# A hybrid four-layer model on one core: the order of every engine from one plan over the whole program

## The chip, the cores and the metric

The kernel runs on one core of a Trainium2 chip. The metric is the device time of one execution in microseconds; the time before is the median of three runs, and one further execution was profiled. The core's engines are TensorE (matrix products), VectorE, ScalarE, GpSimd and SyncE, which here issues DMAs. Each works through its own queue in order; semaphores tie them together.

## The reference

A sequence of 256 tokens, 1024 wide, in float32, goes through two blocks of two layers each. Both layers of the first block project the normalised x to the inputs of three mixers (a recurrence, an attention over 64 selected keys, dilated attention), multiply their joined output by `w_out`, and then add a gated projection of a second input `p`:

```
for i in range(2):                                   # first block
    z = rms_norm(x, norm_g[i]) @ w_in[i]
    y = concat(rwkv7(z_a), sparse_attention(z_b), dilated(z_c))
    x = x + y @ w_out[i]
    x = x + sigmoid(rms_norm(x, ple_norm_g[i]) @ ple_w_gate[i]) * (p[i] @ ple_w_proj[i])
x = rms_norm(x, final_norm_g)
for l in range(2):                                   # second block
    h = rms_norm(x, attn_norm[l])
    o = compressed/selected/window attention (l = 0) or attention with decay (l = 1), and attention to mem
    x = x + o @ w_o[l]
    u = conv3(rms_norm(x, ffn_norm[l]) @ w_up[l]) + conv_b[l]      # 2 x 2816 columns
    x = x + (silu(u[:, :2816]) * u[:, 2816:]) @ w_down[l]
return rms_norm(x, final_norm)
```

The recurrence of `rwkv7` (six heads, a 64 x 64 state each) is computed in four chunks of 64 tokens.

## The kernel before

**Products.** A float32 product is made of three products in a faster type: each operand x is split into a high half (a rounded copy) and a low half (x minus the copy), and hi·hi, hi·lo and lo·hi are added in PSUM (`mm3`, `PASSES`). TensorE therefore gets three matmuls of 128 x 128 weights by 256 or 512 columns for each tile of a projection. Small products (attention, the recurrence, transposes) run as plain float32.

**Weights.** A `Load` brings weights from DRAM through a ring of three raw tiles of 512 KB (`wraw`, `RBUFS`). ScalarE writes the high half of each block (`whi`), VectorE or, for every n-th block, GpSimd the low half (`wlo`); each has a ring of six (`WBUFS`). `Chain`s link the loads, so that the next projection's weights are fetched and split while the current one runs. Activations are split in the same way (`put_pair`, `stack_row`); in the feed-forward stage GpSimd makes the low half of the gated product (`k<-yv,k`).

**Stages.** `flow.run(...)` is called nine times: mixers and gated projection for each layer of the first block, mixers and feed-forward for each layer of the second, and the last norm. A call takes several Python generators (streams): the dense projections, the norms' statistics, the recurrence, the attentions. The feed-forward stage has 11 passes a layer, each with two up-projections of 256 columns and the down-projection of the pass before.

**Order of TensorE.** Streams are interleaved by `Flow`, which keeps a clock of its own: `Clock` estimates when VectorE, ScalarE, GpSimd and DMA finish each operation (`RATE`), and `Flow.run` resumes the first stream in its list whose operands it thinks are ready. A stream that has handed work over waits for it with a margin: `PACE` holds, for each of the nine calls, a margin of 0.15 to 0.6 us and a lag between TensorE and the others of 0.2 to 0.28, and three places add 2.0 to 3.5 us (`GN_LAG`, `GRAM_LAG`, `SPREAD_LAG`). The order in which this program emits matmuls is kept as it is by `tc.manual_schedule(engines={PE})` (line 494).

**Order of the other engines.** VectorE, ScalarE, GpSimd and SyncE are ordered by the framework's scheduler, which has estimates of its own (`schedule_with_timeline_sim=True`). It also gives each tile a slot of its pool and places the semaphores.

**The norms.** Row sums of squares give 1/rms by three Newton steps on [128, 1] tiles, mostly on GpSimd (`newton`: `rs_t`, `rs_y`). `spread_rs` spreads the two columns of scales over the partitions: VectorE writes a diagonal tile (`diag`), and TensorE multiplies it by ones.

Nearly every instruction has the line of a helper: 458 for all engines but TensorE, 616 for matmuls, 621 for transposes.

## Time and profile before

| what | us |
|---|---|
| median of three runs (1206.95 to 1211.45) | 1207.41 |
| the profiled execution | 1210.38 |
| its span, first to last instruction | 1208.6 |
| TensorE, matmuls busy | 1111.5 |
| TensorE, weight loads busy (beside the matmuls) | 988.7 |
| VectorE busy | 913.0 |
| ScalarE busy | 716.8 |
| GpSimd busy | 363.8 |
| mean granted clock of TensorE | 0.959 |

In the profile's names PE is TensorE's matmuls, PEld its weight loads, DVE VectorE, ACT ScalarE, POOL GpSimd, SP SyncE (SPq its queue of DMAs). A tile is named without its number; `k` stands for many tiles. The end of a matmul is modelled, and matmuls overlap, so the mean duration of one is longer than its share of the busy time. The granted clock of 1 is 2.4 GHz, of 0.5 is 1.2 GHz.

### The profile page before, as it was taken

The numbers are of one execution on the slowest core, as the hardware profiler recorded it, in microseconds if no ns is written. First come the engines' busy times: TensorE is split into PE (matmuls) and PEld (weight loads), VectorE is DVE, ScalarE is ACT, GpSimd is POOL, SyncE is SP. The second block draws the span as 40 slices with busy tenths as digits, with TensorE's granted clock in tenths as the row PEclk, the third lists the DMA queues.
The fourth block names the chain that finished last, engine by engine and source line by source line (L and its number), as shares of the span: only waits on it lengthen the run. The fifth ranks groups of instructions, "written<-read, shape, count | busy, mean of one in ns | idle before, by whom it ended". The sixth has DMA issues, their size and how long they took to land.

```text
span 1208.6 us, 23379 instructions
## 1 busy us (share of the span) xinstructions
PE 1111.5 (92%) x8485; PEld 988.7 (82%) x8485; DVE 913.0 (76%) x2229; ACT 716.8 (59%) x1625; POOL 363.8 (30%) x357
## 2 busy tenths in 40 slices
PE   6889999988989989978979899999989998999996
PEld 5888887888888867976847899999778867999995
DVE  4888887778898877866677578777776766877886
ACT  4525656655266666665565566666565555766664
POOL 4452213433521226150001522122351124222221
PEclk8989999999799999989989899999999998999999
DMA  7444224454452146646312466566534334666662
GB/s 209 117 126 122 80 53 140 141 140 119 113 139 81 45 135 214 181 129 208 113 30 81 143 183 182 184 198 189 173 105 132 115 90 141 191 192 190 181 187 89
DMA packets 154124, 168.54 MB, mean 139 GB/s; under 512 B 15722, under 2 KB 141562, under 8 KB 154008
## 3 DMA queue, kind: packets, MB, share of 16 engines
q1 hardware_dynamic: 153336, 166.10, 46.4%
q0 software_dynamic: 672, 0.95, 0.4%
q8 instruction: 67, 1.10, 0.4%
q14 instruction: 49, 0.40, 0.1%
HBM read 164.59 MB, written 2.42 MB: 138 GB/s over the span
## 4 chain that ended last, share of the span: by engine, by line
PE 62%; issue 13%; DVE 10%; POOL 7%; ACT 4%; DMA 3%; SPq 0%; ACTq 0%; POOLq 0%; DVEq 0%
PE pz L616 33%; PE po L616 9%; PE pr L616 7%; PE sc L616 6%; POOL k L458 4%; PE tp L616 3%; PE tp L621 2%; DVE k L458 2%; DVE wlo L458 2%; POOL wlo L458 2%; ACT whi L458 2%; POOL rs_t L458 1%; ACT k L458 1%; DMA wraw<-in_w_in_dram 1%; DVE sm L458 1%
## 5 line engine op out<-in xcount | busy, mean ns | idle before, releaser
L458 ACT ACTIVATE whi<-wraw 128x512 fp32r<-128x512 f32 (+3 forms) x588 | 361.5, 624 | 246.7 <-PE pz L616 74.2
L458 DVE TENSOR_TENSOR wlo<-wraw,whi 128x512 fp32r<-128x512 f32 (+1 forms) x489 | 352.9, 734 | 148.7 <-ACT whi L458 139.8
L616 PE MATMUL pz<-k,whi 128*128 128x256 f32 x1568 | 313.4, 296 | 7.8 <-ACT k L458 5.3
L616 PEld LDWEIGHTS pz<-k,whi 128*128 128x128 f32 x1568 | 255.1, 199 | 18.0 <-issue 5.7
L458 POOL TENSOR_TENSOR wlo<-wraw,whi 128x512 fp32r<-128x512 f32 (+3 forms) x99 | 133.6, 1351 | 416.5 <-ACT whi L458 360.9
L616 PE MATMUL pz<-whi,k 128*128 128x256 f32 (+4 forms) x1088 | 233.7, 301 | 8.0 <-DVE k L458 5.4
L616 PE MATMUL pz<-k,wlo 128*128 128x256 f32 x784 | 228.8, 292 | 9.6 <-POOL wlo L458 9.6
L616 PEld LDWEIGHTS pz<-whi,k 128*128 128x128 f32 x1088 | 178.8, 191 | 18.5 <-DVE k L458 7.2
L458 POOL TENSOR_TENSOR k<-yv,k 128x256 fp32r<-128x256 f32 x54 | 97.1, 1813 | 280.6 <-ACT k L458 280.6
L616 PEld LDWEIGHTS pz<-k,wlo 128*128 128x128 f32 x784 | 156.7, 200 | 11.2 <-POOL wlo L458 11.1
L616 PE MATMUL pz<-wlo,k 128*128 128x256 f32 (+4 forms) x544 | 160.6, 295 | 0.0
L616 PE MATMUL po<-k,whi 128*128 128x256 f32 x704 | 132.5, 281 | 0.0
L616 PEld LDWEIGHTS po<-k,whi 128*128 128x128 f32 x704 | 109.1, 191 | 0.0
L616 PEld LDWEIGHTS pz<-wlo,k 128*128 128x128 f32 x544 | 104.3, 192 | 2.2
L616 PE MATMUL po<-k,wlo 128*128 128x256 f32 x352 | 99.0, 281 | 0.0
L616 PE MATMUL sc<-whi,k 128*128 128x512 f32 x240 | 82.3, 403 | 3.5 <-POOL k L458 3.1
L458 DVE SCALAR_TENSOR_TENSOR k<-zs,convp,k 128x254 f32<-128x254 f32 (+1 forms) x176 | 73.3, 476 | 0.0
L616 PEld LDWEIGHTS po<-k,wlo 128*128 128x128 f32 x352 | 67.1, 190 | 0.0
L458 ACT ACTIVATE sm<-sm,mn 128x128 f32<-128x128 f32 x100 | 44.4, 445 | 32.2 <-DVE mn L458 31.9
L616 PE MATMUL tp<-whi,k 128*128 128x512 f32 x176 | 58.8, 395 | 0.0
L616 PEld LDWEIGHTS sc<-whi,k 128*128 128x128 f32 x240 | 45.5, 190 | 15.4 <-POOL k L458 4.2
L616 PE MATMUL sc<-wlo,k 128*128 128x512 f32 x120 | 47.9, 399 | 0.0
(381 smaller groups left out, 1850.0 us busy)
## 6 DMA issues: line engine op xcount, KB each, us to landing
wraw<-in_w_up_dram SPq DMA_DIRECT2D x88, 512.0 KB
wraw<-in_w_in_dram SPq DMA_DIRECT2D x44, 512.0 KB
wraw<-in_w_down_dram SPq DMA_DIRECT2D x44, 512.0 KB
wraw<-in_w_in_dram SPq DMA_DIRECT2D x32, 256.0 KB
wraw<-in_w_out_dram SPq DMA_DIRECT2D x16, 512.0 KB
wraw<-in_ple_w_gate_dram SPq DMA_DIRECT2D x16, 512.0 KB
wraw<-in_w_o_dram SPq DMA_DIRECT2D x10, 512.0 KB
wraw<-in_w_kv_shared_dram SPq DMA_DIRECT2D x10, 512.0 KB
```

The costliest lines, as they stand in the source:

```text
L458: ins = call(*args, **kw)
L616: nc.tensor.matmul(out_, st, mv, start=start, stop=stop)
L621: nc.tensor.transpose(out_, x, idn)
```

## The change

`Flow` and its streams emit the same instructions as before. Beside that, every instruction is now recorded as a `Node` in a `Plan`, with its engine, an estimated cost, the instructions it depends on (overlapping reads and writes; in a PSUM bank also the last use by another engine) and the tiles it uses. Tiles of a kind (a pool's tag) begin in the order of emission and no more of them at a time than the kind has buffers.

When all is recorded, `settle` runs two rounds. `forward` is a list scheduler: it advances a modelled time, and whenever an engine is free it takes, of the instructions that are ready on it, the one of lowest rank. It models the lock between GpSimd and VectorE instructions that read two tiles of SBUF (`port`), ScalarE's function tables, the DMAs as one server, and TensorE's clock. In the first round the rank is the place in the emission; then `backward` runs the program in reverse, and an instruction's rank in the second round is the time at which it is needed by that. Of the two orders the one with the shorter modelled span is kept, and every instruction is tied to the one before it on its engine by an edge without a semaphore. `manual_schedule` for TensorE is dropped. Cut to its core:

```diff
@@ Flow.note, Flow.product
+            node = self.plan.add(issuer, 0.45 if issuer == "SP" else 1.0, reads, writes, ins, issuer != "SP", cost)
+        else:
+            port = lane == "POOL"
+            if lane == "DVE" and n > 2:
+                big = [x for x in reads if x.space != PSUM and math.prod(x.shape[1:]) > 1]
+                port = len(big) > 1 or name in ("tensor_scalar", "tensor_copy") and len(big) == 1 and writes[0].space != PSUM
+            node = self.plan.add(lane, cost, reads, writes, ins, port)
...
+    def product(self, ins, passes, out, st, mv):
+        n, m = math.prod(mv.shape[1:]), math.prod(st.shape[1:])
+        node = self.plan.add("PE", 0.0, (st, mv), (out,), ins)
+        if passes == 1 and mv.dtype != F32 and n >= 256:
+            node.cycles, node.share = n * 1.09, 1 / 1.09
...
@@ class Plan
+    @staticmethod
+    def lag(a, b):
+        if a == "JOIN" or b == "JOIN":
+            return 0.0
+        if a == "SP" or a == "DMA":
+            return 1.3
+        if a == "PE":
+            return 0.0 if b == "PE" else 0.24
+        if b == "PE":
+            return 0.22
+        return 0.13 if a == b else 0.17
...
+    def forward(self, rank):
...
+        def stuck(n):
+            for tile in n.tiles:
+                if tile.kind is not None and tile not in began and (begun[tile.kind] != tile.nth or room[tile.kind] <= 0):
+                    return tile.kind
+            return None
...
+            t, lane = best
...
+            _, i = heapq.heappop(q)
+            n = self.nodes[i]
+            kind = stuck(n)
+            if kind is not None:
+                blocked[kind].append(n)
+                continue
...
+    def settle(self, tc):
+        self.close()
+        best = None
+        rank = {n: n.i for n in self.nodes}
+        for _ in range(self.ROUNDS):
+            span, order = self.forward(rank)
+            if best is None or span < best[0]:
+                best = (span, order)
+            ends = self.backward({n: n.end for n in self.nodes})
+            top = max(ends.values())
+            rank = {n: top - e for n, e in ends.items()}
+        best[1].pop("JOIN")
+        for lane, nodes in best[1].items():
+            for a, b in zip(nodes, nodes[1:]):
+                tc.add_manual_dep(b.ins, a.ins.name, mybir.DependencyInfo(mybir.DependencyClass.NoSync, mybir.DependencyReason.DATA),
+                                  reason="order of the plan")
+
+    ROUNDS = 2
@@ tile_hybrid_stack
-    ctx.enter_context(tc.manual_schedule(engines={mybir.EngineType.PE}))
...
+        flow.plan.settle(tc)
```

## Rows read from the trace of the kernel before

**Rows 1.** The page's head: span; busy time of each engine, share, instructions.

```profile
span 1208.6 us, 23379 instructions
PE 1111.5 (92%) x8485; PEld 988.7 (82%) x8485; DVE 913.0 (76%) x2229; ACT 716.8 (59%) x1625; POOL 363.8 (30%) x357
```

**Rows 2.** By stage: stretch, length, busy of five engines, clock, DMA share, GB/s.

```profile
0.00:264.00 264.00, 232.61 (x1938) 207.16 (x1939) 205.72 (x523) 147.42 (x355) 92.75 (x99) 0.94 0.46 129
264.00:527.00 263.00, 246.18 (x2083) 221.21 (x2082) 215.45 (x542) 154.23 (x372) 98.61 (x117) 0.95 0.44 125
527.00:681.00 154.00, 135.85 (x992) 108.22 (x993) 106.82 (x376) 92.30 (x256) 28.48 (x39) 0.96 0.39 113
681.00:868.00 187.00, 183.36 (x1306) 172.17 (x1304) 138.47 (x259) 118.13 (x219) 46.09 (x26) 0.98 0.60 184
868.00:1004.00 136.00, 124.59 (x835) 103.89 (x835) 92.91 (x239) 78.62 (x190) 43.32 (x43) 0.96 0.39 117
1004.00:1191.00 187.00, 182.76 (x1315) 171.74 (x1313) 143.86 (x267) 121.13 (x225) 51.82 (x35) 0.98 0.57 175
1191.00:1209.00 18.00, 6.14 (x26) 4.35 (x24) 9.76 (x30) 4.98 (x12) 2.68 (x2) 0.83 0.15 59
...
0.00:30.00 30.00, 19.62 (x106) 17.56 (x107) 13.58 (x31) 14.36 (x33) 14.89 (x25) 0.83 0.70 208
```

**Rows 3.** Waits of TensorE's matmuls: total us, times, longest.

```profile
PE pz L616 <- POOL wlo L458: 9.6, 7, 3.4
...
PE pz L621 <- DMA row<-in_norm_g_dram: 5.1, 1, 5.1
```

**Rows 4.** Timeline: start, us, instruction, idle before and its end; 45 to 53, and 299.

```profile
45.13 5.63 POOL L458 TENSOR_TENSOR k<-kz,ppx 64x256 f32<-64x256 f32 x4 [4.52 <-DVE kz L458]
46.86 1.18 ACT L458 ACTIVATE whi<-wraw 128x512 fp32r<-128x512 f32 x2 [0.29 <-DMA wraw<-in_w_in_dram]
50.84 1.59 POOL L458 TENSOR_TENSOR wlo<-wraw,whi 128x512 fp32r<-128x512 f32 x1
52.48 0.58 PE L616 MATMUL pz<-k,wlo 128*128 128x256 f32 x1 [3.44 <-POOL wlo L458]
...
299.43 0.58 PE L616 MATMUL pz<-k,wlo 128*128 128x256 f32 x1 [3.42 <-POOL wlo L458]
```

**Rows 5.** Timeline, 262 to 264 us.

```profile
262.64 0.51 DVE L458 TENSOR_SCALAR omm<-prm 128x13 f32<-128x13 f32 x1
...
263.82 0.52 PE L621 MATMUL pr<-cst,x 128*128 128x128 f32 x2 [4.44 <-DVE rs_y L458]
```

**Rows 6.** Timeline, 532 and 685 us.

```profile
532.22 0.80 PE L616 MATMUL po<-diag,ones 128*128 128x128 f32 x2 [4.47 <-DVE diag L458]
...
685.26 0.79 PE L616 MATMUL po<-diag,ones 128*128 128x128 f32 x2 [3.64 <-DVE diag L458]
```

**Rows 7.** Waits of TensorE's weight loads: total us, times, longest.

```profile
PEld pz L616 <- issue: 8.8, 31, 0.6
```

**Rows 8.** The recurrent stretches, columns as in rows 2.

```profile
30.00:180.00 150.00, 136.79 (x1303) 124.29 (x1303) 129.44 (x349) 79.92 (x195) 50.08 (x43) 0.93 0.38 101
300.00:420.00 120.00, 114.28 (x1133) 103.54 (x1132) 102.31 (x302) 62.45 (x161) 37.41 (x32) 0.92 0.38 99
```

**Rows 9.** Groups by form: busy us, mean ns; idle before, what ended it.

```profile
L458 DVE TENSOR_TENSOR wlo<-wraw,whi 128x512 fp32r<-128x512 f32 x471 | 339.8, 734 | 144.0 <-ACT whi L458 135.1 <-PE pz L616 5.7 <-PE po L616 1.3
...
L458 POOL TENSOR_TENSOR k<-yv,k 128x256 fp32r<-128x256 f32 x54 | 97.1, 1813 | 280.6 <-ACT k L458 280.6
...
L458 ACT ACT_TABLE_LOAD x6 | 7.7, 1283 | 0.8 <-PEq L2532 0.7
```

**Rows 10.** Waits of SyncE's DMA queue: total us, times, longest.

```profile
SPq L458 <- DVE wlo L458: 673.9, 223, 15.5
```

**Rows 11.** The chain in order of time: start, us, what; two feed-forward passes.

```profile
727.75 2.78 PE sc L616 x12
...
744.61 2.78 PE sc L616 x12
```

More of the change, by code (lines that the diff above doesn't have):

```diff
@@ L1 @@
+import heapq
 import math
@@ L325, in __init__ @@
         self.table = AF.Exp
+        self.plan = Plan()
         self.quiet, self.issue, self.lanes, self.work = False, 0.0, [0.0] * 4, {}
@@ L340, in note @@
             table = {AF.Ln: AF.Ln, AF.Silu: AF.Silu, AF.Exp: AF.Exp, AF.Tanh: AF.Exp}.get(func, self.table)
-            if table != self.table:
-                self.table = table
-                cost += 1.28
+            late = table != self.table
+            self.table = table
             cost += 0.13 * (len(writes) - 1) + 0.045 * (len(reads) - 1)
@@ L346, in note @@
             cost += 0.09 * (len(reads) - 1)
+        if lane == "DMA":
+            node = self.plan.add(issuer, 0.45 if issuer == "SP" else 1.0, reads, writes, ins, issuer != "SP", cost)
[5 more added lines that the diff above has]
+            node = self.plan.add(lane, cost, reads, writes, ins, port)
+            if lane == "ACT":
+                node.table = self.plan.TABLES.get(func)
+                if late:
+                    cost += 1.28
         self.clock.now = self.t
@@ L350, in note @@
             self.cur.ops.append(op)
+    def product(self, ins, passes, out, st, mv):
[3 more added lines that the diff above has]
+            node.cycles, node.share = n * 1.09, 1 / 1.09
+        else:
+            node.cycles, node.share = passes * (2 * max(n, m) + 6), n / max(n, m)
+        node.share *= st.shape[0] / P
+        r0, r1, c0, c1 = (x // 32 for ap in (st, out) for x in (Clock.region(ap)[1], Clock.region(ap)[2] + 31))
+        node.cells = tuple(4 * r + c for r in range(r0, r1) for c in range(c0, c1))
     def tensor(self, cycles, out, st, mv):
@@ L445, in run, with __init__ @@
                 self.t = self.issue = t
+class Node:
+    __slots__ = ("i", "lane", "cost", "ins", "port", "deps", "after", "tiles", "users", "table", "cells", "cycles", "share",
+                 "dma", "left", "ready", "start", "end", "key", "rank")
+    def __init__(self, i, lane, cost, ins):
+        self.i, self.lane, self.cost, self.ins = i, lane, cost, ins
+        self.port, self.deps, self.after, self.tiles, self.users = False, {}, set(), [], []
+        self.table, self.cells, self.cycles, self.share, self.dma = None, (), 0, 0.0, 0.0
@@ L578, in T @@
         flow.clock.belongs(x.name, id(pool))
+        flow.plan.tile(x.name, (id(pool), tag), bufs, pool=id(pool))
         if tag in FIFO:
@@ L593, in take @@
         flow.clock.belongs(ps.name, "psum")
+        flow.plan.tile(ps.name, (len(phase["banks"]), tag), phase["banks"][tag], True, ("psum", len(phase["banks"])))
         return ps, (times, i, ps.name)
@@ L615, in matmul @@
         flow.tensor(n if mv.dtype != F32 and n >= 256 else 4 * (max(n, 64 + n // 2) if m > 64 else n), out_, st, mv)
-        nc.tensor.matmul(out_, st, mv, start=start, stop=stop)
+        flow.product(nc.tensor.matmul(out_, st, mv, start=start, stop=stop).ins, 1 if mv.dtype != F32 else 2, out_, st, mv)
     def transpose(out_, x, idn=None):
@@ L620, in transpose @@
         flow.tensor(2 * x.shape[0], out_, x, idn)
-        nc.tensor.transpose(out_, x, idn)
+        flow.product(nc.tensor.transpose(out_, x, idn).ins, 1, out_, x, idn)
     def tt(out_, x, y, op, eng=None):
@@ L722, in fetch @@
             flow.clock.new(raw.name, "wraw", RBUFS)
+            flow.plan.tile(raw.name, "wraw", RBUFS)
             rv = raw[:, :kt * n].rearrange("p (k n) -> p k n", k=kt)
@@ L748, in loading @@
                     flow.clock.new(x.name, tag, WBUFS)
+                    flow.plan.tile(x.name, tag, WBUFS)
                 hv, lv = (x[:, :w].rearrange("p (k n) -> p k n", k=b.kn) for x in (hi, lo))
@@ L2444, in swap @@
             flow.clock.follows(id(p_), id(phase["pools"][0][0]))
+            flow.plan.follows(id(p_), id(phase["pools"][0][0]))
         phase["pools"][0] = phase["mem"]
@@ L2511, in tile_hybrid_stack @@
         flow.clock.follows(id(pool), first)
+        flow.plan.follows(id(pool), first)
+        flow.plan.follows(("psum", len(BANKS_2)), ("psum", len(BANKS_1)))
         cst.append(T([P, cuts[4] - cuts[3]], "cst3"))
```

215 lines of the change are left out of this document (added).

## The prediction

> **What bounds the kernel now.** I read the page first: TensorE is the busiest engine by far, 1111.5 us of a span of 1208.6, VectorE follows with 913.0 [rows 1]. Next I cut the span into stages and took each engine's busy time in each [rows 2]; the DMA engines' share there is 0.39 to 0.60, so bandwidth is not the bound, and only what shortens TensorE's day counts. The reader is to see two kinds of stage. In the two feed-forward stages (681 to 868 and 1004 to 1191) TensorE idles 3.6 and 4.2 us of 187: no order can help there. In the four mixing stages it idles 31.4, 16.8, 18.2 and 11.4 us, with the last 18 us another 11.9. The seven sum to 97.5 us, of which the first 30 us of the span hold 10.4.
>
> Third, the waits by engine: GpSimd's low halves of weight blocks head the list with 9.6 us in 7 waits, and the largest for a DMA is one of 5.1 us at the very start [rows 3]. Fourth, I looked at the longest waits in order of time, asking each time whether the thing waited for could have been made earlier, or something else done meanwhile:
> - Around 52 us TensorE waits 3.44 us for a low half of a weight block. GpSimd makes it, but in its queue four products of the recurrence stand ahead of it, 5.63 us long; ScalarE had the high half ready at 48.04 [rows 4]. With only the product that GpSimd has begun to wait out, the split starts near 48.1, not at 50.84: 2.7 us are in the order. The second layer repeats it at 299.43 [rows 4].
> - Around 263.8 us TensorE waits 4.44 us to transpose x; VectorE (the row names rs_y, which it ends just after) makes a parameter column (0.51 us) and its like before the last update of x, while a dense product that waits for nothing stands behind the transposes [rows 5].
> - At 532.22 and 685.26 us TensorE waits 4.47 and 3.64 us for the small diag tile of a norm, whose scale comes through a chain of short GpSimd steps that are mixed with splits [rows 6]. The dense products behind it then run without a wait: the diag product stood too early in TensorE's order.
>
> So the five longest waits, 3.44 + 3.42 + 4.44 + 4.47 + 3.64 = 19.4 us, are faults of order. TensorE's order is fixed by one program (the emission with its own clock), that of the other engines by another (the framework's scheduler), and where the two disagree TensorE stands.
>
> **The change part by part.** *No work is added or removed.* The edges are between instructions of one engine and carry no semaphore. What may change is the number of waits that have to be spelled out; the trace has no row for one that is already met, the nearest is TensorE's weight load held up by "issue", 31 times, 8.8 us [rows 7]. Between nothing and as much again (0 to +8.8 us; less than none has no cause, since an already fixed order is replaced by another), I take 0, as most of these lie in idle time anyway.
>
> *TensorE's order comes from the plan.* Idle 97.5 us; the first 30 us hold 10.4 (nothing is normalised yet) and the last 18 us 11.9 (the final norm); both are dependency, not order. That leaves 75.2. Of the 19.4 us of long waits I take three quarters back: 2.7 of 3.44 at the GpSimd cases, nearly all of the diag cases, some two thirds at 263.8, where the low halves of the normalised x are late next. That is 14.5. The other 55.8 us are short waits; there the thing late next is often only tenths behind, and tiles of a kind still begin in the order of emission, so weight blocks and accumulators can't overtake each other. I take 40%, 22.3 us. Together 36.8. The ends are 0 and 75.2.
>
> *The clock.* The granted clock is 0.92 to 0.96 in the mixing stages and 0.98 in the others [rows 2, 8], lowest in the recurrent stretches, where TensorE works on small products between waits; the two levels are 1.2 and 2.4 GHz. The mean over the span, 0.959, leaves 49.6 us of full clock not granted; 8.2 of it are in the first 30 and last 18 us. Of the other 41.4 some 90% falls on time in which TensorE works (739 of 817 us in the mixing stages). With half of the idle time gone I take a third of the dips as gone too, since small products stay what they are: 41.4 x 0.9 / 3 = 12.4 us (ends 0 and 37).
>
> *VectorE, ScalarE, GpSimd by need.* They get no faster: a low half takes VectorE 734 ns in any order [rows 9]. ScalarE loads a function table six times, 1283 ns each [rows 9]; the plan counts a load but does not avoid one, so where it mixes stages there can be more: none to six more, 0 to 7.7 us, beside TensorE's work as ScalarE has slack; I take 0. In the two recurrent stretches VectorE is busy 129.4 of 150 and 102.3 of 120 us [rows 8]; better order can close at most the other 38 us there, which the terms above contain.
>
> *SyncE's queue.* Every weight load and every small load (parameter rows, constants, the bounce of the recurrence) is moved to its place by need; so are GpSimd's own few DMAs, behind which its splits queue. Weight loads wait for their ring, 673.9 us in total for a low half of VectorE [rows 10], not for bandwidth. A small load may now stand behind such a wait. Gain in the first 30 us, at most the 5.1 us for which TensorE waits on a gain row [rows 3]; loss, as much again. I take 0.
>
> *New waits.* The emission gave every hand-over a margin, 0.15 to 0.6 us by stage, and before three steps 2.0 to 3.5 us. The plan has a fixed lag and no margin, so a product that comes later than it thinks holds the whole engine. The price goes by the short waits of today: 55.8 us in some 108 waits of the list, 0.52 each. I take 20 new ones, 10 us (ends 0 and 108 of them, 56).
>
> Sum: 36.8 + 12.4 - 10 = 39.2 us. The profiled execution took 1210.4 us, 1.8 more than its span, so 1171.2; the median of the runs is 3.0 lower, so 1168.
>
> A rule of the Trainium skill bears on the ceiling. TensorE's load row is idle 220 us, not 97.5 [rows 1, 2]. Perfetto Trace Analysis, Identifying the Most-Contended Engine, says that the matmul row is a bad measure of headroom, since matmuls are pipelined, and that the busy share of LDWEIGHTS is the good one. By the matmul row the sum is the one above; by the load row it is the first rival. The trace bears it out in part: in the feed-forward stages the load row still idles 15 us of 187 with hardly a wait.
>
> **The rivals.**
> 1. *The headroom is the load row's.* It idles 56.8, 41.8, 45.8 and 32.1 us in the mixing stages [rows 2], 176.5 in all, less 12.4 in the first 30 us: 164. Much of the difference is short stalls inside what counts as busy. At the share of 49% that I gave the waits (36.8 of 75.2), 80 us come back; 80 + 12 - 10 = 82, 1125. Against it: small products of 64 rows and columns have short loads, and the row idles there at any order.
> 2. *The chains bind.* VectorE at 86% in the recurrent stretches [rows 8] and the norms' chains leave TensorE nothing else to do; the order is new, the waits move. Then only the long waits return and the new ones take most of it: 14.5 - 10, 4.5 us, 1203.
> 3. *The plan changes little.* It keeps the better of two orders by its own clock, and the first of them ranks by emission. Or the framework gives rings out in another order than the plan assumed. Then about 1207.
> 4. *The feed-forward passes lose their lead (slower).* Today a pass takes 16.86 us [rows 11] and no operand is late: splits are made as soon as a ring slot is free, a pass ahead. Ranked by need, a split may be left until just before its product. If in each of the 22 passes one GpSimd split (1.81 us) and one of VectorE (0.73) [rows 9] end up in series before a product, that is 2.54 x 22 = 56 us: 1168 + 56 = 1224. It decides from 39 / 22 = 1.8 us a pass on. For it: VectorE is busy 138.5 of 187 us there [rows 2]. Against it: the forward pass never leaves an engine idle that has something ready, and GpSimd has 46.1 of 187.
>
> **How the numbers follow.** Forecast 0.50, rival 1 0.16, rival 2 0.08, rival 3 0.04, rival 4 0.22. A measurement of this kernel tells about 0.5% (6 us) from no change. Faster: 0.50 + 0.16 = 0.66; same: 0.08 + 0.04 = 0.12; slower: 0.22. For the range I leave out what of rival 1 goes on below 1112, about half (0.08), and the upper half of rival 4 (0.11): 1112 to 1226. The forecast's own range, from some 1.3 times its gain and the clock's upper end to a third of it, is 1132 to 1195.
>
> **What would show it.** TensorE's idle time near 60 us, the granted clock near 0.97, the five waits named above gone and no wait over 2 us outside the first 30; busy times of the other engines within 2%, and feed-forward passes still 16.9 us long. Passes of 18 us or more show rival 4; idle time near 95 with other names in it shows rival 2; an idle load row near 140 us shows rival 1. The prediction is wrong in its base if the waits that I call faults of order stay although the order changed.

## The result: slower, and the profile after

The changed kernel took 1254.99 us (median of four runs, 1250.37 to 1261.91), the kernel before 1209.43 beside it: a ratio of 1.0381, 95% interval 1.0316 to 1.0446. The forecast was 1168, its range ended at 1226. Both the sign and the range are wrong.

The page's head of the changed kernel, to be read against [rows 1]:

```profile
span 1249.3 us, 23412 instructions
PE 1175.2 (94%) x8485; PEld 1014.9 (81%) x8485; DVE 898.7 (72%) x2229; ACT 719.4 (58%) x1625; POOL 315.6 (25%) x357
```

TensorE runs the same 8485 matmuls. Its idle time fell, as forecast, from 97.1 us (1208.6 - 1111.5) to 74.1. But its busy time rose from 1111.5 to 1175.2: the same products took 64 us longer.

Where? Here are both kernels cut at the same marks of the work (the transposes of x that open a stage), before and then after; columns as in [rows 2]. The first two rows are the layers of the first block, the third and fifth the mixers of the second block, the fourth and sixth its feed-forward stages.

```profile
0.00:257.00 257.00, 230.19 (x1922) 205.43 (x1922) 198.76 (x506) 142.78 (x344) 89.28 (x95) 0.94 0.45 128
257.00:506.00 249.00, 229.01 (x1941) 204.13 (x1939) 203.12 (x522) 144.56 (x349) 87.07 (x97) 0.95 0.43 124
506.00:670.00 164.00, 144.45 (x1058) 116.05 (x1059) 117.81 (x399) 100.34 (x279) 34.26 (x54) 0.96 0.40 115
670.00:878.00 208.00, 202.21 (x1426) 188.89 (x1425) 151.59 (x281) 128.91 (x242) 61.35 (x39) 0.98 0.58 179
878.00:1003.00 125.00, 115.89 (x805) 97.55 (x803) 87.08 (x227) 73.14 (x178) 36.30 (x38) 0.97 0.39 117
1003.00:1199.00 196.00, 189.75 (x1344) 176.71 (x1342) 150.28 (x281) 124.89 (x234) 55.50 (x38) 0.98 0.55 168
```

```profile
0.00:276.20 276.20, 251.45 (x1920) 215.34 (x1921) 189.17 (x506) 143.13 (x344) 86.27 (x95) 0.94 0.42 118
276.20:533.60 257.40, 237.82 (x1943) 206.23 (x1941) 197.24 (x522) 145.66 (x350) 86.91 (x97) 0.95 0.42 121
533.60:702.60 169.00, 159.69 (x1054) 121.57 (x1055) 113.65 (x397) 100.78 (x279) 35.40 (x54) 0.95 0.39 111
702.60:901.40 198.80, 197.40 (x1418) 184.79 (x1417) 152.82 (x279) 126.15 (x235) 37.35 (x38) 1.00 0.60 184
901.40:1043.00 141.60, 134.26 (x808) 106.63 (x807) 87.28 (x229) 75.65 (x182) 35.43 (x36) 0.93 0.34 105
1043.00:1241.00 198.00, 194.62 (x1350) 180.36 (x1348) 154.32 (x286) 125.91 (x237) 34.20 (x39) 0.98 0.54 168
```

The four mixing stages grew by 19, 8, 5 and 17 us, and in each of them TensorE's busy time grew (by 21, 9, 15 and 18), with the count of matmuls unchanged within 4. The feed-forward stages together are 7 us shorter. So the loss is in products of the mixing stages that take longer, not in waits.

Which products: the four groups, by form, of attention scores (`sc`) and of probabilities times values (`po<-pt`), in the kernel before and in the changed one; after the bar the busy time, then the mean length of one.

```profile
L616 PE MATMUL sc<-k,k 64*128 64x256 f32 x92 | 17.4, 379 | 0.0
L616 PE MATMUL sc<-k,k 64*128 64x128 f32 x92 | 14.7, 323 | 0.9 <-ACT k L458 0.7 <-DVE mn L458 0.2
L616 PE MATMUL po<-pt,k 128*64 128x256 f32 x72 | 13.8, 419 | 1.3 <-ACT pt L458 1.1
L616 PE MATMUL po<-pt,k 128*64 128x128 f32 x72 | 8.5, 282 | 0.0
```

```profile
L941 PE MATMUL sc<-k,k 64*128 64x256 f32 x92 | 26.3, 415 | 0.0
L941 PE MATMUL sc<-k,k 64*128 64x128 f32 x92 | 21.0, 336 | 1.8 <-DVE mn L782 1.6
L941 PE MATMUL po<-pt,k 128*64 128x256 f32 x72 | 20.4, 417 | 0.8 <-ACT pt L782 0.8
L941 PE MATMUL po<-pt,k 128*64 128x128 f32 x72 | 14.1, 301 | 0.0
```

The length of one product differs little (379 and 415 ns), the busy time of the group far more: 54.4 us for the four groups before, 81.8 after. These products use 64 of the array's 128 rows or columns, and two of them, one for each head of a pair, run on the two halves at once if they stand next to each other in TensorE's queue. The timeline shows it: first eight such products of the kernel before, then four of the changed one (start, length from the first start to the last end, count). Each row merges equal numbers of products of 128 and of 256 columns.

```profile
568.90 0.93 PE L616 MATMUL sc<-k,k 64*128 64x128 f32 x8
569.75 0.24 PE L621 MATMUL tp<-cst,kd 30*128 30x30 f32 x1
```

```profile
593.46 0.92 PE L941 MATMUL sc<-k,k 64*128 64x128 f32 x4
594.31 0.30 PE L941 MATMUL pz<-cw,chid 128*30 128x64 f32 x2
```

Eight products take as long as four: 0.85 us to the next start in both. In the kernel before they start in pairs 7 ns apart (568.897 and 568.904, 569.110 and 569.117, and so on); in the changed one they start singly, 0.214, 0.111, 0.219 and 0.306 us after one another. A lone half-array product costs what a pair costs. That two tiles of the array work at once, and that matmuls start and end strictly in the order of the queue, is what the Trainium skill says (TensorE: Matmul & The Clock Gate, Part 3: Packing small matmuls — row/col tiling). The trace agrees with the first in the starts 7 ns apart; it can't show the second by itself, since the ends of matmuls are modelled in it. What it shows is that the pairs which the new order parted ran apart.

To size this over the whole program I took the intervals between the starts of consecutive matmuls from each trace; one of over 0.75 us counts as a gap, every other is put to the product that begins it. "Beside" counts half-array products (1768 in all) that started within 0.03 us of the half-array product ahead of them; "changes" counts steps from a large product (of the split operands, fp32r) to a small float32 one.

| kernel | median us | half-array us | beside | other small us | large us | gaps us | changes |
|---|---|---|---|---|---|---|---|
| before | 1209 to 1211 | 150.0 | 797 | 82.1 | 871.6 | 89.4 | 152 |
| changed | 1254.99 | 191.9 | 633 | 81.7 | 896.0 | 66.3 | 273 |
| e3_pe_as_emitted | 1230.16 | 154.8 | 801 | 81.0 | 871.8 | 102.9 | 152 |
| e4_pe_plan_alone | 1287.77 | 202.4 | 597 | 89.1 | 898.6 | 80.1 | 273 |
| e2_one_round | 1245.12 | 181.6 | 662 | 82.1 | 881.3 | 80.3 | 260 |
| e1_pairs | 1202.37 | 148.4 | 819 | 80.2 | 882.3 | 72.0 | 257 |
| e6_half_pairs | 1231.74 | 175.9 | 695 | 81.4 | 885.9 | 74.2 | 248 |
| e10_before_by_head | 1220.17 | 154.0 | 790 | 86.4 | 871.3 | 92.2 | 150 |
| e5_runs | 1216.28 | 155.0 | 815 | 89.0 | 879.7 | 78.1 | 223 |
| e7_pairs_rings | 1186.40 | 151.4 | 803 | 81.0 | 883.5 | 55.6 | 247 |
| e14_rings_pe_alone | 1233.17 | 156.4 | 744 | 81.1 | 881.3 | 96.0 | 247 |
| e11_rings_one_round | 1217.67 | 149.7 | 809 | 83.6 | 876.0 | 83.0 | 236 |
| e15_few_switches_4 | 1194.34 | 149.5 | 826 | 86.1 | 869.3 | 71.7 | 198 |
| e15_few_switches_8 | 1198.97 | 152.1 | 810 | 90.5 | 866.7 | 73.0 | 130 |

From before to changed: half-array products +41.9, other small ones -0.4, large ones +24.4, gaps -23.1, in sum +42.8 (the spans differ by 40.7; the first start and the last end are not in the intervals). 164 products that ran beside another no longer do, 41.9 / 164 = 0.256 us each. The columns are of the one profiled execution of each kernel, the medians of all its executions. Ratios leave out executions over 1.5% above the fastest of their kernel; these are three of the ten of e12_rings_margin, its profiled one among them, so it has no row here.

A lower clock is not the reason. In the stretches of full granted clock alone, an interval that begins with one of the attention products above is 0.107 us long on average before and 0.180 in the changed kernel.

### The profile page after: what moved, and what is told of

It is laid out like the page before. It is cut to its first block, busy times and chain, and to the rows that moved or that the text cites. A ratio compares the mean times of both kernels' runs of the same rounds, so it can differ in the third digit from the quotient of the medians.

```text
span 1249.3 us, 23412 instructions
## 1 busy us (share of the span) xinstructions
PE 1175.2 (94%) x8485; PEld 1014.9 (81%) x8485; DVE 898.7 (72%) x2229; ACT 719.4 (58%) x1625; POOL 315.6 (25%) x357
## 4 chain that ended last, share of the span: by engine, by line
PE 76%; DVE 7%; ACT 5%; issue 2%; DMA 2%; POOL 1%; SPq 0%; ACTq 0%; POOLq 0%; DVEq 0%
PE pz L941 37%; PE po L941 13%; PE sc L941 10%; PE pr L941 7%; PE tp L941 5%; PE tp L946 3%; ACT whi L782 2%; ACT k L782 2%; DVE wlo L782 1%; DVE k L782 1%; DMA wraw<-in_ple_w_gate_dram 1%; PE sc L946 1%; DVE zs L782 1%; PE pr L946 1%; DVE r L782 1%
## 5 line engine op out<-in xcount | busy, mean ns | idle before, releaser
L782 DVE TENSOR_TENSOR wlo<-wraw,whi 128x512 fp32r<-128x512 f32 (+1 forms) x489 | 342.7, 714 | 158.6 <-ACT whi L782 149.4
L941 PE MATMUL pz<-whi,k 128*128 128x256 f32 (+4 forms) x1088 | 245.5, 311 | 14.9 <-ACT k L782 11.2
L941 PEld LDWEIGHTS pz<-whi,k 128*128 128x128 f32 x1088 | 184.5, 199 | 26.2 <-ACT k L782 12.2
L941 PE MATMUL pz<-wlo,k 128*128 128x256 f32 (+4 forms) x544 | 168.5, 310 | 0.4 <-DVE wlo L782 0.4
L941 PEld LDWEIGHTS pz<-k,wlo 128*128 128x128 f32 x784 | 154.0, 197 | 5.6 <-DVE wlo L782 3.1
L782 POOL TENSOR_TENSOR k<-yv,k 128x256 fp32r<-128x256 f32 x54 | 52.2, 968 | 334.6 <-ACT k L782 285.9
L941 PEld LDWEIGHTS pz<-wlo,k 128*128 128x128 f32 x544 | 107.7, 198 | 6.9 <-issue 2.6
L782 DVE SCALAR_TENSOR_TENSOR k<-zs,convp,k 128x254 f32<-128x254 f32 (+1 forms) x176 | 84.2, 524 | 0.0
L941 PE MATMUL sc<-k,k 64*128 64x128 f32 (+2 forms) x216 | 49.7, 368 | 1.9 <-DVE mn L782 1.6
```

The costliest lines, as they stand in the source:

```text
L782: ins = call(*args, **kw)
L941: flow.product(nc.tensor.matmul(out_, st, mv, start=start, stop=stop).ins, 1 if mv.dtype != F32 else 2, out_, st, mv)
```

## The experiments

Four theories stood against each other. P: the plan's order parts half-array pairs and changes more often between large and small products; what it costs is TensorE's own time. B: the backward pass finds when an instruction is needed by its users, but not that its end frees a buffer that a later tile waits for; what it costs is waits. M: the plan leaves no margin, so each operation that is a little late holds TensorE. O: the new order of the other four engines is at fault. Kernels run together share their runs of the kernel before (1209.87, 1210.73, 1210.82 and 1210.35 us in four groups).

**Which engine's order?** e3_pe_as_emitted leaves TensorE in the order of emission and plans the rest around it; e4_pe_plan_alone ties TensorE alone to the plan.

```diff
+        tensor = [n for n in self.nodes if n.lane == "PE"]      # e3
+        for a, b in zip(tensor, tensor[1:]):
+            b.after.add(a)
...
+            if lane != "PE":                                      # e4, in settle
+                continue
```

> The changed kernel, but the plan must keep TensorE's products in the order of emission, as the kernel before has them; the other four engines are ordered by the plan. Theory P: no pair is split, so the 35 us of small products are back; TensorE waits again where the emission misjudged the others, 1200 to 1220. Rival M: the emission's margins are in TensorE's order again, 1200 to 1215, and the small products must not matter. Rival O: it stays at 1240 or more, since the other engines' order is the plan's.

> The changed kernel, but only TensorE is tied to the plan's order; the other four engines are ordered by the framework's scheduler, as before the change. Theory P: the pairs are still split, so the small products cost their 35 us more than before and the engines agree less: 1250 or more. Rival O: the other engines are as before, so the time returns to 1205 to 1225. Rival M: 1250 or more, with more waits of TensorE.

Measured: e3 1230.16 us, ratio 1.0200 (1.0148 to 1.0251); e4 1287.77, ratio 1.0650 (1.0613 to 1.0687). With the emission's order of TensorE the half-array products are back (154.8 us, 801 beside another) and the changes too (152), so these follow TensorE's order alone. What e3 loses, 20 us by the medians, lies between the bands of P and O; its profiled execution is 15 us behind that of the kernel before, 13.5 of them gaps. So the order of the other engines costs something too. But it is not the loss: e4 has their old order and, of two executions, the longest time and the dearest products of all (202.4), as P and M said. Each half of the change by itself is slower than the kernel before.

**Which ranking?** e2_one_round sets `ROUNDS = 1`: the ranks are the places of emission, and the backward pass is not used.

> The changed kernel with the first round alone: no ranking by need, the plan takes of what is ready the product emitted first. Theory P: fewer pairs are split than by need (both members were emitted side by side), but those whose operands come one after the other still are, so the time lies between: 1215 to 1245, with the small half-array products between the two kernels' times. Rival M: no margin here either, so 1245 to 1260. Rival O: if ranking by need is what is wrong with the other engines' order, 1205 to 1220.

Measured: 1245.12 us (two executions), ratio 1.0297 (1.0261 to 1.0334), at the border of P's band and M's, with half-array products between the two kernels' as P said. Even ranked by emission the forward pass parts pairs (662 beside another), because it takes whatever is ready the moment TensorE is free; ranking by need parts 29 more and saves 14 us of gaps (80.3 to 66.3).

**The pairs put back.** e1_pairs is the changed kernel, with every unbroken run of half-array products in the emission kept unbroken: its members share their dependencies and the earliest rank, and begin only when the banks of all are free.

```diff
+            half = node is not None and node.lane == "PE" and len(node.cells) < 16
+            if half and (not run or node.i == run[-1].i + 1):
+                run.append(node)
+                continue
...
+        for run in self.groups:
+            outer = dict.fromkeys(d for n in run for d in n.deps if d not in run)
+            for n in run:
+                n.deps.update(outer)
+                self.group[n] = run
...
+            for run in self.groups:
+                first = min(rank[n] for n in run)
+                for n in run:
+                    rank[n] = first
```

> The changed kernel with one addition to its plan: small products that use half of the array and are emitted one right behind the other (a run) become ready together, share one rank and begin only when the banks of all of them are free. Everything else is planned as before. Theory P (the loss is that products on the two halves of the array no longer stand side by side): the matmuls of 64 rows by 256 and of 128 by 64 columns lose the some 35 us that they gained in the changed kernel, and the time falls from 1255 by 30 to 45 us, to 1210 to 1225. Rival M (the plan has no margin, and late operands hold TensorE): pairs made whole change at most 10 us, 1245 to 1255. Rival O (the new order of VectorE, ScalarE, GpSimd and SyncE is at fault): the same, 1245 to 1255.

Measured: 1202.37 us, ratio 0.9936 (0.9908 to 0.9965). That is 52.6 us below the changed kernel and more than theory P had asked for. The half-array products fell from 191.9 to 148.4 us, the large ones from 896.0 to 882.3, and the gaps rose by 5.7. By form, the same four groups as above:

```profile
L964 PE MATMUL sc<-k,k 64*128 64x256 f32 x92 | 19.5, 409 | 0.0
L964 PE MATMUL sc<-k,k 64*128 64x128 f32 x92 | 15.5, 342 | 2.2 <-DVE mn L805 1.8 <-ACT k L805 0.3
L964 PE MATMUL po<-pt,k 128*64 128x256 f32 x72 | 14.5, 405 | 1.5 <-ACT pt L805 1.5
L964 PE MATMUL po<-pt,k 128*64 128x128 f32 x72 | 8.4, 277 | 0.0
```

57.9 us, against 81.8 in the changed kernel and 54.4 before.

**Half the dose, and the reverse.** e6_half_pairs keeps every second run (`self.groups = self.groups[::2]`). e10_before_by_head parts the pairs in the kernel before, with no plan at all: in `scores` and `pv` both products of a head come ahead of those of the other.

```diff
         for e, (qT, kT) in enumerate(pair):
             matmul(got[e][0][:, 0:P], qT[:, 0:P], kT[:, 0:P])
-        for e, (qT, kT) in enumerate(pair):
             matmul(got[e][0][:, P:P + S], qT[:, P:S], kT[:, 0:S])
```

> The kernel of e1_pairs, but only every second run of half-array products is kept unbroken (26 adjacent pairs in pv and 24 in scores, against 52 and 36 in the kernel before, 14 and 8 in the changed one). Theory P: about half of the 52 us that e1_pairs gained over the changed kernel, so 1223 to 1235 us, and the time of half-array products between 150 and 192 us, near 172 us. Theory that e1_pairs gained by its waits alone (a tied run enters TensorE later, when its inputs are there) and not by overlap: no proportion to the pairs; the time of half-array products near 190 us or near 150 us, not between.

> The kernel before, without any plan: in scores and in pv the two products of the first head are emitted ahead of the two of the second head (they alternated between the heads). Nothing else differs. Theory P: the four products of a quartet go from two overlapped pairs (0.33 us in the trace of the kernel before) to one, two overlapped, one (about 0.11 + 0.22 + 0.22 = 0.55 us), on some 26 quartets of scores and 26 of pv: 6 to 12 us more, 1216 to 1222 us, and the time of half-array products rises from 150 us to about 160 us. If the order of the heads costs nothing by itself and the changed kernel lost elsewhere: within 3 us of the kernel before.

Measured: e6 1231.74 us, ratio 1.0192 (1.0155 to 1.0229); e10 1220.17, ratio 1.0090 (1.0063 to 1.0116). e6 lies in the middle, and its half-array products fall on the line of the two ends: 695 run beside another, 102 fewer than before, 150.0 + 102 x 0.256 = 176.1 us; measured 175.9. Near it lie e2 (184.6 by the line, 181.6 measured) and e4 (201.2 and 202.4), which were not built for it; further off e14_rings_pe_alone below (163.6 and 156.4) and e5_runs (145.4 and 155.0). The attention products alone, at full clock, give the same order: 0.107 us for an interval before, 0.103 in e1, 0.137 in e6, 0.164 in e2, 0.180 in the changed kernel, 0.184 in e4.

e10 loses 9.4 us, within P's band, but not where P said: half-array products +4.0 us with only 7 fewer beside another (the second product of one head now runs beside the first of the other), other small products +4.3, gaps +2.8. At full clock its attention products kept 0.107 us; but 114 half-array products began at a granted clock of 0.5, against 66 before, and the mean clock was 0.949 to 0.956 in its four executions, against 0.957 to 0.966 in the nine of the kernel before beside them. So the order of these few lines alone costs time, but e10 is no evidence for the overlap; the dose of e6 and the return in e1 are. What in that order lowers the clock is open.

**What is left waits for buffers.** After the pairs were back, the longest waits of e1_pairs were of the changed kernel's kind again (5.1 and 4.3 us for `zs`, 5.3 for `k`). Those of the changed kernel (total, times, longest), and its single waits of over 2 us outside the first 30 us:

```profile
PE pz L941 <- ACT k L782: 14.0, 8, 4.1
PE pz L941 <- DVE zs L782: 9.0, 2, 5.1
```

```profile
69.86 0.77 PE L941 MATMUL pz<-k,whi 128*128 128x256 f32 x2 [3.90 <-DVE zs L782]
...
249.31 0.39 PE L941 MATMUL pz<-whi,k 128*128 128x256 f32 x1 [2.48 <-ACT k L782]
...
334.05 0.79 PE L941 MATMUL pz<-k,whi 128*128 128x256 f32 x2 [5.09 <-DVE zs L782]
...
503.61 0.58 PE L941 MATMUL pz<-whi,k 128*128 128x256 f32 x1 [3.77 <-ACT k L782]
...
552.34 0.77 PE L941 MATMUL po<-diag,ones 128*128 128x128 f32 x2 [3.73 <-DVE diag L782]
...
910.83 0.59 PE L941 MATMUL pz<-whi,k 128*128 128x268 f32 x1 [4.14 <-ACT k L782]
```

The two waits for `zs` are for a PSUM bank (`zs` is what VectorE reads out of it, not an operand of the product); those for ScalarE's `k` are for an operand, as far as I followed them. VectorE's queue ahead of 334.05:

```profile
328.01 1.27 DVE L782 TENSOR_TENSOR ad<-pr,cst 64x512 f32<-64x512 f32 x2
329.21 2.20 DVE L782 TENSOR_TENSOR wlo<-wraw,whi 128x256 fp32r<-128x256 f32 x2
331.44 0.69 DVE L782 TENSOR_TENSOR ad<-pr,cst 64x512 f32<-64x512 f32 x1
332.17 1.11 DVE L782 TENSOR_TENSOR wlo<-wraw,whi 128x256 fp32r<-128x256 f32 x2
333.31 0.69 DVE L782 TENSOR_TENSOR zs<-pz,wide 128x512 f32<-128x512 f32 x1
```

TensorE had filled the bank by about 329. VectorE first ends one product of the recurrence and makes another and four half blocks of weights, because, as I read the plan, what it reads out of the bank is needed late by its own users; that the next tile needs the bank is in no rank. e7_pairs_rings puts it there: for each tile that begins when its ring is full, the release of the tile that ends first counts as needed by it.

```diff
+                if len(live) == self.kinds[kind][1]:
+                    old = min(live, key=lambda t: t.nodes[-1].i)
...
+                                self.frees.setdefault(first, []).append(n)
+                                self.takes.setdefault(n, []).append(first)
...
+            for d in self.frees.get(n, ()):
+                at[d] = max(at[d], end + self.lag(d.lane, lane))
+                left[d] -= 1
...
```

> The kernel of e1_pairs, and the backward pass also counts that a tile's buffer is wanted by the tile that takes its place in the ring: the release counts as needed by that tile's first instruction. Theory B: the waits of TensorE for bank pz behind ScalarE and VectorE (rows of 12.0 and 10.1 us in e1_pairs) fall to under 8 us together, and the time to 1185 to 1195 us. Theory P: overlap and changes between products stay as they are, so the time stays within 5 us of e1_pairs, 1197 to 1207 us; the waits move to other tiles. Theory M: as P, the waits for late operations stay at 20 us and more in sum whatever the ranks.

Measured: 1186.40 us (1182.44 to 1188.45), ratio 0.9802 (0.9775 to 0.9830). This beats both kernels: 24 us below the one before, 69 below the changed one. Gaps fell from 72.0 in e1_pairs to 55.6 us, the products stayed (+5 us in sum), as B said. Its waits that answer to the two rows above, and its single waits over 2 us outside the first 30:

```profile
PE pz L983 <- ACT k L824: 8.3, 5, 3.0
...
PE pz L983 <- DVE zs L824: 2.1, 1, 2.1
```

```profile
318.71 0.40 PE L983 MATMUL pz<-whi,k 128*128 128x296 f32 x1 [2.06 <-DVE zs L824]
...
592.87 0.48 PE L983 MATMUL sc<-k,k 64*128 64x128 f32 x2 [2.65 <-DVE mn L824]
...
861.39 0.59 PE L983 MATMUL pz<-whi,k 128*128 128x268 f32 x1 [3.01 <-ACT k L824]
```

The row for `zs` was 9.0 us in the changed kernel and 10.1 in e1_pairs; it is 2.1 now. With the row for `k` (12.0 in e1_pairs) the sum went from 22.1 to 10.4 us, not quite to the under 8 that B had named: part of that row was, as far as I followed it, no wait for a bank. The buffers without the pairs were not tried.

**What carries the gain of e7_pairs_rings?** Three cuts: e11_rings_one_round ranks by emission (`ROUNDS = 1`), e14_rings_pe_alone ties TensorE alone (the edit of e4), e12_rings_margin adds 0.3 us to the plan's lag between engines.

```diff
-            return 0.0 if b == "PE" else 0.24
+            return 0.0 if b == "PE" else 0.54
...
-            return 0.22
-        return 0.13 if a == b else 0.17
+            return 0.52
+        return 0.13 if a == b else 0.47
```

> The kernel of e7_pairs_rings, with one round of the plan: the ranks are the places in the program's order, and what the backward pass finds (when each instruction is needed) is not used. If need-ranks are worth something once half-array products are kept together and buffers are counted: some 10 to 20 us above e7_pairs_rings, 1196 to 1206 us. If the gain over the kernel before is from the forward pass alone (an operation is placed when its inputs are ready): within 4 us of e7_pairs_rings, 1182 to 1190 us. In the changed kernel itself the same cut made it 10 us shorter, which would give about 1177 us.

> The kernel of e7_pairs_rings, but only TensorE is tied to the plan; VectorE, ScalarE, GpSimd and SyncE are ordered as in the kernel before. With the changed kernel this cut cost 33 us (e4_pe_plan_alone), while the prediction gave the order of these engines nothing. If their order matters since TensorE's order is fixed against theirs: 20 to 40 us above e7_pairs_rings, 1206 to 1226 us, as waits of TensorE for VectorE and ScalarE. If it was the split of half-array products that made the changed kernel sensitive to it: within 10 us, 1186 to 1196 us.

> The kernel of e7_pairs_rings, with 0.3 us more allowed in the plan for the step from one engine to another (0.54 and 0.52 us for steps from and to TensorE, 0.47 us between others). Theory M (products are put right behind the operation that they wait for, and each slip stalls TensorE): gaps of over 0.75 us between matmul starts fall from 55.6 us to under 45 us, and the time to 1172 to 1182 us. Theory that the gaps left come from chains with nothing else to do: gaps stay within 5 us and the time within 5 us of 1186 us.

Measured: e11 1217.67 us, ratio 1.0068 (1.0041 to 1.0095); e14 1233.17, ratio 1.0192 (1.0170 to 1.0215); e12 1203.17 (1201.62 without the three), ratio 0.9908 (0.9876 to 0.9940). Ranking by need, which lost 10 us in the changed kernel, is worth 31 here by the medians, more than any band written for it. The profiled execution of e11 is the fastest of its ten (1209.92), so the traces hold only 21 of the 31: 27 us of gaps (83.0 to 55.6) less 7 of large products. Need-ranks saved gaps in the changed kernel too (14 us), but there they parted more pairs. The order of VectorE, ScalarE, GpSimd and SyncE is worth 47 us once TensorE's is fixed by the plan, again more than the band (20 to 40); without it the gaps are 96.0, and most lie in many short waits:

```profile
PE pz L985 <- ACT k L826: 11.0, 7, 2.2
PE sc L985 <- ACT k L826: 7.7, 7, 2.5
PE pz L985 <- POOL wlo L826: 7.0, 4, 4.0
PE pr L985 <- DVE k L826: 6.5, 8, 1.8
```

A margin of this size makes it 15 us worse (1201.62 against 1186.40), so theory M falls in this form; both of the bands written for e12 lie below what it took.

**The changes between large and small products.** e5_runs widens the rule of e1_pairs to any run of small products; e15_few_switches_8 and _4 let TensorE, in the plan, take a ready product of the present kind first if its need is at most 8 or 4 us later (on top of e7_pairs_rings).

```diff
-            half = node is not None and node.lane == "PE" and len(node.cells) < 16
+            half = node is not None and node.lane == "PE" and node.small        # e5
...
+            if lane == "PE" and n.small != small:                               # e15
+                for r, j in sorted(q):
+                    if r > _ + 8.0:
+                        break
+                    if self.nodes[j].small == small and stuck(self.nodes[j]) is None:
...
+                        n = self.nodes[j]
+                        break
```

> The kernel of e1_pairs, with the rule widened: any unbroken run of small float32 products in the program's order (transposes, whole-array products and half-array products alike) stands unbroken in TensorE's order. The plan's order then has 447 changes from a large product to a small one, against 515 in e1_pairs and 305 rows of the kernel before. Theory P (what the plan's order costs is overlap of half-array products and, second, the changes between large and small products): 68 changes fewer at 0.08 to 0.1 us each, so 5 to 9 us below e1_pairs: 1193 to 1198 us. Theory M (the plan's order has no margin, so products wait for the operation that was due just ahead of them): a run waits for the latest input of all its products, so more waits: 1205 to 1215 us. Theory B (what is left are waits for PSUM banks that the backward pass doesn't see): about as e1_pairs, 1200 to 1205 us.

> The kernel of e7_pairs_rings; where the plan's next product would change TensorE from large fp32r products to small float32 ones or back, a ready product of the present kind is taken first if its need is at most 8 us later. Rows of change in the order: 261 against 495 (the kernel before has 305). Theory that the changes carry part of the loss: 117 changes from large to small fewer at 0.085 us (0.207 us from a large product's start to a small one's against 0.121 us to another large one) are 10 us: 1174 to 1180 us. Rival, what a change costs is given back as the array leaves the small products, and a need put off by up to 8 us makes other engines late: no gain in the sum of the products, more gaps, 1190 to 1215 us.

> As e15_few_switches_8, with needs put off by at most 4 us: 397 rows of change against 495. Theory that the changes carry part of the loss: 49 changes fewer at 0.085 us are 4 us: 1180 to 1184 us. Rival: 1186 to 1200 us, between e7_pairs_rings and e15_few_switches_8.

Measured: e5 1216.28 us, ratio 1.0045 (1.0019 to 1.0071); e15_few_switches_8 1198.97, ratio 0.9894 (0.9845 to 0.9943); e15_few_switches_4 1194.34, ratio 0.9864 (0.9828 to 0.9900). All three are slower than what they were built on. e5 lies above every band written for it: with 34 changes fewer than e1, its other small products took 8.8 us more, its half-array ones 6.6, its gaps 6.1. Both e15 runs lie in the bands of their rival. In e15_few_switches_8 the large products took 16.8 us less than in e7_pairs_rings with 117 changes fewer, but the other small products took 9.5 more: a whole-array transpose that is followed by another small product takes longer to the next start (0.136 us) than one followed by a large product (0.051). Net, products gained 6.6 us (16.8 - 9.5 - 0.7), 0.06 us a change, and the gaps rose by 17.4. By that price the 121 additional changes of the changed kernel are some 7 us of its loss, an estimate; no run has taken them away by themselves, and of the 24.4 us that its large products gained e1_pairs gave back 13.7 with only 16 changes fewer. About half of the 13.7 is clock: 233 large products of the changed kernel began at a granted clock of 0.5, 182 of e1_pairs, at some 0.09 to 0.10 us each over those at full clock, some 7.5 us in sum. The rest stays unexplained. Of the 24.4 itself an estimate puts some 12 us at the steps from a large product to a half-array one (at full clock 70 before, 140 in the changed kernel, each 0.09 to 0.14 us dearer than a step to another large one).

## Why the prediction was wrong, point by point

**"No work is added or removed": the step that failed.** It counted instructions and took each one's time as its own, at a cost of 0. The time of a half-array product depends on its neighbour in the queue, so an order by itself adds or removes busy time: TensorE's rose by 63.7 us. Half-array products are 41.9 of it, and with the pairs kept together all of that came back (43.5 in e1_pairs); the large products' 24.4 are explained in part only. It could have been read from the trace of before: 92 products of 379 ns each are busy for 17.4 us, 0.19 us each. I read rows of waits and of idle time, and took 1111.5 us of busy time as a constant [rows 1]. The 0 to 8.8 us that this step did allow were for another thing, waits spelled out, and these are not the loss: TensorE has 158 instructions for waits before, 176 in the changed kernel, and 179 in e7_pairs_rings, the fastest. The 8.8 us were also only one of seven rows of weight loads held up by "issue": together 33.2 us before, 57.8 in the changed kernel and 32.5 in e1_pairs, so their growth was gone with the pairs put back.

**"TensorE's order comes from the plan" (36.8 us): right in sign, under two thirds of the size.** Idle time fell by 23.0 us (97.1 to 74.1), gaps by 23.1, not to near 60. Both of its terms gave some two thirds. Of the five long waits [rows 4 to 6] four are gone and one for a diag tile remains (3.73 us at 552.34), where I had said that all five would go; and five new waits of 2.5 to 5.1 us came. All single waits of over 2 us outside the first 30 were 32.1 us in ten before and are 23.1 in six: 9 us, where I took 14.5 from five of them and expected no others (the parts of the 14.5, as worded, come to some 16). The rest, 14 us of 23, is short waits, where I took 22.3. e7_pairs_rings shows what two of the new ones came from: needs that don't count buffers. With that mended, gaps fell by 33.8 us against before, and the forecast's 36.8 is nearly there.

**"The clock" (12.4 us): nothing, if not a loss.** The mean granted clock of the profiled execution is 0.957, against 0.959 before, though idle time fell; the other three of the changed kernel have 0.948 to 0.954, where the executions of the kernel before beside the experiments have 0.955 to 0.968. e7_pairs_rings has 0.963. The first feed-forward stage went to 1.00, the second layer's mixers from 0.97 to 0.93. It does not follow the idle time in the way that I assumed.

**"VectorE, ScalarE, GpSimd by need" (0): a real term.** Function tables are still loaded six times, and VectorE's and ScalarE's busy times are within 2%. But their order carries much: planned around an unchanged TensorE it cost 20 us (e3), and under e7's order of TensorE it is worth 47 (e14). Costing it at nothing was right only in that it makes no operation shorter, and not even that held for GpSimd (below).

**"SyncE's queue" (0): held.** The wait of 5.1 us for a gain row [rows 3] is no longer among the rows; one of 4.5 us for the constants stands at the start in its place. No wait of TensorE for a DMA outside the first 30 us reaches 2 us.

**"New waits" (10 us): present, of another kind.** I had priced short slips. What came were five long ones, 19.4 us, two for a bank and three, as far as I followed them, for an operand; and a larger margin made e7_pairs_rings worse (e12).

**Rival 1, the load row's headroom.** Refuted as put: the load row is idle 234 us (1249.3 - 1014.9), not near 140. The rule of the Trainium skill behind it (Perfetto Trace Analysis, Identifying the Most-Contended Engine: judge by MFU and LDWEIGHTS, not by the matmul row) pointed at the right doubt, since the matmul row read 94% busy in the slower kernel; but the load row did not give the headroom either. In e7_pairs_rings it idles 199 us, 21 less than before, with a gain of 24.

**Rivals 2 and 3.** Idle time is 74 us, not 95, and the order is new: neither.

**Rival 4, slower.** Right sign, wrong mechanism. The chain shows feed-forward passes at 16.89 us in the first such stage, against 16.86 [rows 11], and 16.98 in the second:

```profile
753.64 2.80 PE sc L941 x12
770.53 2.80 PE sc L941 x12
...
1093.25 2.79 PE sc L941 x12
1110.23 2.79 PE sc L941 x12
```

The splits kept their lead. The range reached to 1226 for a loss of lead; it had no case in which products themselves get dearer, and so the time fell outside it.

## What to carry to other kernels

Before an order is left to a plan, ask of each engine whether an instruction's time depends on its neighbours: compare a group's busy time with count times mean, and if partners share the engine, give the plan the group and not its members. A need-driven order must also count the release of a buffer as needed by whoever takes the buffer next. And try an order's parts on all engines together: here TensorE's plan alone, and the others' alone, were each slower than no plan.

## What the runs showed of the hardware that was not expected

A half-array float32 product that stands alone costs as much of TensorE's time as a pair: eight in pairs 0.85 us, four alone 0.85 us, 0.256 us for each partner lost over the program.

A whole-array transpose followed by a large product had the next start after 0.051 us, one followed by another small product after 0.136; the step from a large product of 256 columns to a small one took 0.207 us, to another large one 0.121 (means at full clock, intervals up to 0.75 us, e7_pairs_rings). So what a change costs on the way in (0.086) is given back on the way out where a transpose is the last of the small products (0.085).

The same intervals split by what follows: from the large product 0.258 us to a half-array product (111 steps), 0.144 to a small product on the whole array (88); from a small product on the whole array 0.232 to a half-array one (29), 0.127 to another on the whole array (477). In these means the dear step is the one onto the half array, whichever type comes before it, rather than the change of type. There are 106 such steps before, 207 in the changed kernel, 172 in e1_pairs and 159 in e7_pairs_rings. No run varied them alone.

GpSimd's low halves of the gated product took 0.97 us each in the changed kernel, against 1813 ns [rows 9]:

```profile
L782 POOL TENSOR_TENSOR k<-yv,k 128x256 fp32r<-128x256 f32 x54 | 52.2, 968 | 334.6 <-ACT k L782 285.9 <-PE po L941 48.5
```

The same 54 instructions are 45 us shorter, most of GpSimd's 48 us. It goes with the plan's order of the engines other than TensorE: their mean is 0.92 us in e3_pe_as_emitted, 1.66 and 1.79 us in the two kernels with TensorE's plan alone (e4_pe_plan_alone, e14_rings_pe_alone). In the kernel before, the 14 that no low half of VectorE's overlapped took 0.745 us, the other 40 took 2.19; in the changed kernel it is 8 at 0.747 and 46 at 1.01. In its modelled time the plan does not let GpSimd run beside a VectorE operation that it marks as using a shared port, which may be the cause; no run takes that rule away. The feed-forward passes did not get shorter by it (16.86 and 16.89 us).
